# Projection stage: posts behind a tile's sums held back for a while, bank copies by priority; scan, sample states and output projection at other places in the order

## The chip, the cores and the metric

The kernel runs on one core of a Trainium2 chip. The metric is the device time of one execution in microseconds (us), as the median of the runs. The engines are named as in the profile: PE (TensorE matmul) and PEld (its weight loads), DVE (VectorE), ACT (ScalarE), POOL (GpSimd) and SP (SyncE), which here issues the transfers between the chip's memory (DRAM) and the on-chip buffer. Sums of matmuls land in banks of PSUM.

## The reference

One layer of a decoder step for 1024 new tokens of one sequence and 8 x 8 tokens of eight running sequences: a half-step SwiGLU FFN, a mixing block with two branches and gates, a second half-step FFN, and a final norm. Cut to what matters here:

```python
def token_mixing(hn, ...):
    proj = hn @ w_in                       # 1024 -> u 1024, z 2048, xbc 3072, dt 32, gates 2048
    u, z, xbc, dt_raw, gate_logits = ...
    branch_pool = pool_mix(u_ext, ...) @ pool_w_out   # mean of the last 2/4/8/16 rows minus u, a 256x256 map per group
    xbc_c, new_conv = causal_conv(xbc, conv_hist, conv_w, conv_b)   # width 4, SiLU
    dt = softplus(dt_raw + dt_bias); A = -exp(a_log)
    y, new_ssm = ssd_scan(xs, dt, A, bm, cm, ssm_h0)  # h_t = exp(dt A) h + dt x B^T, y = h C, by chunks of 128
    y = rmsnorm per group of ((y + d_skip * xs) * silu(z)) * ssd_norm
    branch_ssd = y @ ssd_w_out
    merged = sigmoid(g0) * branch_pool + sigmoid(g1) * branch_ssd
    return merged @ w_o, new_pool, new_conv, new_ssm

x = x + 0.5 * swiglu(rmsnorm(x), ffn1_w_in, ffn1_w_out)
x = x + mix
x = x + 0.5 * swiglu(rmsnorm(x), ffn2_w_in, ffn2_w_out)
```

All inputs and outputs are float32.

## The kernel before

**Numbers.** Float32 products are made of three matmuls of rounded halves: a value is split into its rounding and the rest (`wh` and `wl` for a weight, `hi`/`lo`, `fh`/`fl`, `mh`/`ml` and so on for an activation). ACT writes the rounding, DVE the rest (L443 and L444, L294 and L295 for weights; L355 and L357 or L359 for activations). Tokens come in two halves: h = 0 has 512 columns, h = 1 has 512 + 64, the 64 of the running sequences.

**Stages.** First FFN up to about 820 us; dt and some gates up to about 880; the projection up to about 1526; the mix (pooling branch, scan, output of the scan, merge, output projection) up to about 2150; second FFN to the end.

**Projection** (`in_proj`, `proj_pair`, lines 1052 to 1170). Columns of `w_in` are taken in pairs of tiles of 128: gates first, then four groups of three conv pairs c, one pooling pair u and two z pairs. A pair is computed by `wino` with seven products of half-size matrices in place of eight (`PRODUCTS`, in the order 1, 2, 6, 5, 7, 3, 4). Products add up in PSUM banks A, B and C of each half, and after each product `after(p, ...)` takes one bank's sums out: ACT copies them (`t` L1104, `v` L1109, `t` L1111 for half 0, L1088 to L1100 for half 1), or DVE or POOL adds them to what is there. A bank that is copied is written by a later product: product 6 needs the copy `t`, product 7 the copy `v`. Weights of some products are sums of weight tiles that POOL makes (L437).

When a tile of the pair is complete, `done()` appends its post-processing to the list `work`: for c the conv (ACT L933, DVE L937, SiLU on ACT L939), for u the window sums (DVE L952, L956, the difference from the mean L963 to L969 and the split of d: ACT `dh` L355, DVE L357), for z and g an activation (ACT L917, L912). A worker, a generator on a side chain, takes the list's first entry whenever it is free, and yields `POST` units between its parts; `proj_pair` steps it until at most three entries are left. `state_out` (transposes `pst` on PE, copies `so` on ACT) writes the new histories.

**Order.** Side chains are generators. Each yields a delay; a clock `pe[0]` of ideal PE time in us advances with the matmuls of the main stream, and `tick()` behind a few matmuls runs the chains whose time has come. The scheduler then puts each engine's instructions in an order of its own by priorities and their modelled readiness; instructions under `tc.high_priority(n)` go ahead by n. On the chip each engine works its queue in order.

**Mix.** `pool_branch` is main stream: a 256 x 256 map per group (`pgm`), then the pool output (`pbp`). Beside it `scan()` goes through groups and chunks by `ssd_group` with a delay `STEP[h]` between parts of a chunk: `ssd_a` (transposes `pxT`, decays `ab` by ACT's exponentials L1342 to L1345 and DVE's mask L1346, products `xdt`, `xd`), `ssd_st` (state sums `pst`), `ssd_b` (`pyd`, `pyo`, outputs; for the running sequences the states: `h0` loaded from DRAM, transposed as `ph0T` to `h0T`, and `pnew`). `sample_parts` makes the running sequences' factors for the states (`px3`, `pb3`). Norms (`rstd`) sum squares by matmul (`pss`). `ssd_out` (`pso`), `merge` (mh, ml) and `out_proj` (`pwo`, added to x at L1619) follow on the main stream for half 0 and then half 1. Two tags of PSUM banks are shared in this stage, "ps" and "pd".

Of the kernel before, what the change touches and what calls it, by code (L numbers as in the profile page):

```python
# [14 lines left out]
P = 128  # L15
# [28 lines left out]
STEP = (5.2, 4.1)  # L44
STEP_S = 1.0
POST = 1.0
GP = (1.0, 1.2)
# [14 lines left out]
def tile_hybrid_pool_ssd_macaron(  # L62
# [306 lines left out]
    def rstd(tiles, h, count, out, pace=1.0):  # L369
# [13 lines left out]
        yield max(pace, 1.5)  # L383
# [443 lines left out]
    def mix_dt(h, xs):  # L827
# [9 lines left out]
        def chain():  # L837
# [32 lines left out]
            yield 12  # L870
# [37 lines left out]
    work, hists, poster = [], {}, [None]  # L908
# [84 lines left out]
    def done(kind, i, h, raw):  # L993

        H, N = BEFORE[kind], NTOK[h]
        if kind in "zg":
            work.append((post_z if kind == "z" else post_gate)(h, i, raw[:, :N]))
            return
# [8 lines left out]
        if kind == "c":  # L1007
            if h == 1:
                smp = new
                state_out(kind, i, raw[:, 512:579])  # L1010
            work.append(post_conv(h, i, raw, smp))
        else:
            if h == 1:
                smp = hists.pop(("u", i))
                G.tensor_copy(smp[0][:, :, HIST:], new)
                state_out(kind, i, raw[:, 512:591])
            work.append(post_u(h, i, raw, smp))
# [6 lines left out]
    def state_out(kind, i, rows_):  # L1024
# [25 lines left out]
        work.append(put())  # L1050

    def proj_pair(kind, ia, ib, xs):
# [3 lines left out]
        while len(work) > 3:  # L1056
            poster[0].step()
        if kind == "u":
# [14 lines left out]
        def after(p, i, bk):  # L1073
# [9 lines left out]
            af, as_, bf, bs = a[:, H : H + n], a[:, H + n : H + 2 * n], b[:, H : H + n], b[:, H + n : H + 2 * n]  # L1083
            A, B, C = bk
# [36 lines left out]
            if p == "3":  # L1121
                done(kind, ia, h, a)
            elif p == "4":
                done(kind, ib, h, b)
# [3 lines left out]
    def in_proj(prep):  # L1128
# [24 lines left out]
        work.append(sample_hist())  # L1153
# [72 lines left out]
    def pool_branch(h):  # L1226
# [11 lines left out]
        for gi in range(4):  # L1238
# [3 lines left out]
            for j, pg in enumerate(dense2(wg[gi], 0, 0, [(h, dh, dl)], ("ps", "ps"), name="pgm")):  # L1242
# [26 lines left out]
    def sample_parts(g, xrs, dtd3):  # L1269

        out = []
        for i, xr in enumerate(xrs):
            px, pb = psum("ps", "px3"), psum("ps", "pb3")
            for j in range(4):
                tr(px[:96, j * P : (j + 1) * P], xr[:, j, :], ident)
            tr(pb[:96, :P], xr[:, 4, :], ident)
            xd, X3 = act((P, 512), name="xd3")[:96], act((P, 512), F32R, "X3")[:96]
            V.tensor_tensor(xd.rearrange("p (h d) -> p h d", d=HD), px[:96, :].rearrange("p (h d) -> p h d", d=HD),
                            dtd3[:, i, g * HPG : (g + 1) * HPG].unsqueeze(2).broadcast_to([96, HPG, HD]), op=ALU.mult)
            S.activation(X3, xd, AF.Copy)  # L1280
            V.tensor_tensor(X3[32:64], xd[32:64], X3[32:64].bitcast(F32), op=ALU.subtract)
            B3 = small((96, P), "B3", 1, F32R)
            S.activation(B3, pb[:96, :P], AF.Copy)
            V.tensor_tensor(B3[64:96], pb[64:96, :P], B3[64:96].bitcast(F32), op=ALU.subtract)
            bb = act((P, 4, P), F32R, "bblk")[:96]
            V.tensor_tensor(bb, B3.bitcast(F32).unsqueeze(1).broadcast_to([96, 4, P]),
                            bsel3.unsqueeze(2).broadcast_to([96, 4, P]), op=ALU.mult)
            out.append((X3, bb))
        return out

    def ssd_a(h, g, c, Bf, Cf, xs4, dts):
# [19 lines left out]
        if smp:  # L1311
            xrs = spread(Bf, xs4)
        yield
# [16 lines left out]
        if smp:  # L1330
            xd = sample_parts(g, xrs, cdp[1])
# [17 lines left out]
    def ssd_b(h, g, c, a, hold, Cf, y4, dts):  # L1349
# [8 lines left out]
        if smp:  # L1358
            units = [(pr, bh) for bh in range(2) for pr in range(4)]

            def src(u):
                gp = g * 4 + u[0]
                return state_ssm[0, u[1] * 4 : u[1] * 4 + 4, 2 * gp : 2 * gp + 2].rearrange("b h p n -> (h p) b n")

            def load(u):
                t = act((P, 4, P), name="h0")
                dma(t, src(u))
                return t
# [9 lines left out]
            h0s = {i: load(units[i]) for i in range(3)}  # L1378
            hTs = {}
            yield STEP_S  # L1380
            for i, (pr, bh) in enumerate(units):
                if i + 3 < len(units):
                    h0s[i + 3] = load(units[i + 3])
# [65 lines left out]
    def ssd_group(h, g, Bf, Cf, xs4, dts, zs):  # L1449
        y4 = xs4  # L1450
        prev = None
        step = STEP[h]
        for c in range(4 + h):
            ga = ssd_a(h, g, c, Bf, Cf, xs4, dts)
# [9 lines left out]
            try:  # L1464
                next(ga)
            except StopIteration as e:
                a = e.value
            yield step
            if prev:
                for w in ssd_b(h, g, *prev, Cf, y4, dts):  # L1470
                    yield w
            prev = (c, a)
        yield step
        for w in ssd_b(h, g, *prev, ssd_st(h, g, *prev, dts), Cf, y4, dts):
            yield w
# [134 lines left out]
    def out_proj(h, mh, ml):  # L1610
        N = NTOK[h]
        out = []
        for m in range(KD):
            x_ = act((P, N), name="x2")
            dma(x_, xspill[h][m])
            pw = dense(w_o[0], 0, KD, m * P, [(h, mh, ml)], name="pwo")[0]
            with tc.high_priority(HP_EV):
                for pt, (a, b) in zip(pw, PIECES[h]):
                    V.tensor_tensor(x_[:, a:b], x_[:, a:b], pt[:, : b - a], op=ALU.add)  # L1619
            dma(xspill[h][m], x_)  # L1620
            if h == 1:
                out.append(x_)
# [139 lines left out]
```

## Time and profile before

| | |
|---|---|
| median of 3 runs | 2939.78 us (2939.3 to 2945.45) |
| profiled execution, its own time | 2943.95 us |
| its span | 2942.2 us (1.75 us lie around it) |
| busy, share of the span | PE 96%, PEld 88%, DVE 60%, ACT 47%, POOL 34% |
| mean granted clock of PE | 0.989 |
| first FFN, 0 to 820 | PE busy 794.13 |
| dt and gates, 820 to 880 | PE busy 56.97 |
| projection, 880 to 1526 | PE busy 628.57, clock 0.99 |
| mix, 1526 to 2150 | PE busy 583.32, clock 0.97 |
| second FFN, 2150 to 2943 | PE busy 773.71 |

A row of the timeline has the start, the duration of one or the extent of several, engine, line, operation, output <- input by the program's names, shapes, count, and in brackets the engine's idle time before it with what ended it. A row of the waits has who waited for whom: total, times, longest. A row of the windows has the window, its length, busy times with numbers of instructions, PE's granted clock (1.00 is full speed), the DMA share and GB/s.

### The profile page before, as it was taken

The numbers are of one execution on the slowest core, as the hardware profiler recorded it, in microseconds if no ns is written. First come the engines' busy times: TensorE is split into PE (matmuls) and PEld (weight loads), VectorE is DVE, ScalarE is ACT, GpSimd is POOL, SyncE is SP. The second block draws the span as 40 slices with busy tenths as digits, with TensorE's granted clock in tenths as the row PEclk, the third lists the DMA queues.
The fourth block names the chain that finished last, engine by engine and source line by source line (L and its number), as shares of the span: only waits on it lengthen the run. The fifth ranks groups of instructions, "written<-read, shape, count | busy, mean of one in ns | idle before, by whom it ended". The sixth has DMA issues, their size and how long they took to land.

```text
span 2942.2 us, 51070 instructions
## 1 busy us (share of the span) xinstructions
PE 2836.7 (96%) x18494; PEld 2575.2 (88%) x18494; DVE 1779.3 (60%) x2843; ACT 1385.2 (47%) x3024; POOL 1001.0 (34%) x1011
## 2 busy tenths in 40 slices
PE   7999999999999999999988999889999999999998
PEld 6999999889989989898977987668999999988898
DVE  6655555434474687887866867865765554453422
ACT  5444444323344555554546656567334444443422
POOL 5444444000133355455522233322225444440000
PEclk9999999999999999999999999999999999999999
DMA  4575554856445455533368677776774432236652
GB/s 125 168 228 183 159 172 133 277 189 195 113 123 171 153 180 160 177 127 122 104 217 253 211 241 236 240 230 196 246 243 155 156 108 74 84 97 215 217 157 72
DMA packets 530332, 507.97 MB, mean 173 GB/s; under 512 B 36884, under 2 KB 374664, under 8 KB 530072
## 3 DMA queue, kind: packets, MB, share of 16 engines
q1 hardware_dynamic: 530064, 504.72, 53.8%
q8 instruction: 145, 2.38, 0.3%
q14 instruction: 107, 0.88, 0.1%
q10 hardware_dynamic: 16, 0.00, 0.0%
HBM read 361.77 MB, written 143.05 MB: 172 GB/s over the span
## 4 chain that ended last, share of the span: by engine, by line
PE 79%; DVE 9%; DMA 4%; ACT 4%; issue 2%; POOL 1%; SPq 1%; DVEq 0%; ACTq 0%; POOLq 0%
PE pw L163 42%; PE po L163 18%; PE pso L163 4%; PE pg L163 3%; PE pwo L163 2%; PE pbp L163 2%; PE pu L163 2%; DVE ct L937 1%; PE pyd L163 1%; DVE wl L444 1%; ACT ab L1344 1%; DMA t<-gd 1%; DVE us L952 1%; PE pst L163 1%; PE pyo L163 1%
## 5 line engine op out<-in xcount | busy, mean ns | idle before, releaser
L163 PE MATMUL pw<-X,wh 128*128 128x288 f32 (+1 forms) x2484 | 624.7, 330 | 12.1 <-ACT v L560 4.3
L163 PE MATMUL pw<-X,wl 128*128 128x288 f32 (+1 forms) x1644 | 474.0, 288 | 3.4 <-DVE wl L444 3.4
L163 PEld LDWEIGHTS pw<-X,wh 128*128 128x128 f32 x2484 | 419.0, 189 | 50.9 <-ACT v L560 5.2
L163 PE MATMUL pw<-hl,wh 128*128 128x512 f32 x1072 | 391.4, 399 | 1.9 <-DVE t L1113 0.9
L444 DVE TENSOR_TENSOR wl<-s,wh 128x512 fp32r<-128x512 f32 x288 | 225.4, 783 | 192.8 <-ACT wh L443 170.9
L163 PE MATMUL pw<-hi,wh 128*128 128x288 f32 x1120 | 331.0, 296 | 1.4 <-ACT t L596 1.3
L163 PE MATMUL pw<-lo,wh 128*128 128x288 f32 x1120 | 329.7, 294 | 0.0
L163 PE MATMUL pw<-hi,wl 128*128 128x288 f32 x1120 | 329.6, 294 | 0.0
L437 POOL TENSOR_TENSOR s<-wraw,wraw 128x512 f32<-128x512 f32 x144 | 206.6, 1435 | 325.3 <-DVE wl L444 216.2
L163 PEld LDWEIGHTS pw<-X,wl 128*128 128x128 f32 x1644 | 311.3, 189 | 5.4 <-DVE wl L444 5.4
L295 DVE TENSOR_TENSOR wl<-wraw,wh 128x512 fp32r<-128x512 f32 x228 | 163.6, 721 | 250.3 <-ACT wh L294 233.2
L163 PE MATMUL pw<-hl,wl 128*128 128x256 f32 x1072 | 299.8, 280 | 2.2 <-DVE wl L444 2.1
L294 ACT ACTIVATE wh<-wraw 128x512 fp32r<-128x512 f32 x228 | 137.7, 607 | 322.8 <-PE po L163 243.9
L444 DVE TENSOR_TENSOR wl<-wraw,wh 128x512 fp32r<-128x512 f32 x216 | 168.9, 782 | 135.5 <-ACT wh L443 127.9
L443 ACT ACTIVATE wh<-s 128x512 fp32r<-128x512 f32 x288 | 181.0, 629 | 139.3 <-PE pw L163 137.0
L163 PEld LDWEIGHTS pw<-hl,wh 128*128 128x128 f32 x1072 | 202.0, 188 | 39.5 <-DVE t L1113 1.4
L163 PEld LDWEIGHTS pw<-hi,wh 128*128 128x128 f32 x1120 | 210.0, 188 | 13.7 <-ACT t L596 1.9
L163 PE MATMUL po<-hh,wh 128*128 128x288 f32 (+1 forms) x800 | 210.9, 323 | 2.9 <-ACT hh L355 2.6
L163 PE MATMUL po<-hr,wh 128*128 128x288 f32 (+1 forms) x800 | 211.1, 323 | 0.0
L163 PE MATMUL po<-hh,wl 128*128 128x288 f32 (+1 forms) x800 | 210.7, 322 | 0.0
L163 PEld LDWEIGHTS pw<-lo,wh 128*128 128x128 f32 x1120 | 210.2, 188 | 0.0
L163 PEld LDWEIGHTS pw<-hi,wl 128*128 128x128 f32 x1120 | 210.1, 188 | 0.0
(384 smaller groups left out, 6346.8 us busy)
## 6 DMA issues: line engine op xcount, KB each, us to landing
wraw<-in_ffn_w_in_dram SPq DMA_DIRECT2D x188, 256.0 KB
wh<-part SPq DMA_DIRECT2D x156, 256.0 KB
wl<-part SPq DMA_DIRECT2D x156, 256.0 KB
wraw<-in_w_in_dram SPq DMA_DIRECT2D x144, 256.0 KB
wraw<-in_ffn_w_out_dram SPq DMA_DIRECT2D x120, 256.0 KB
part<-ph SPq DMA_DIRECT2D x80, 256.0 KB
part<-pr SPq DMA_DIRECT2D x80, 256.0 KB
ab<-acsd SPq DMA_DIRECT2D x64, 256.0 KB
```

Of the source, the lines that this page charges most:

```text
L163: T.matmul(out, lhsT, rhs, start=start, stop=stop, skip_group_check=free)
L294: S.activation(wh, raw, AF.Copy)
L295: V.tensor_tensor(wl, raw, wh.bitcast(F32), op=ALU.subtract)
L437: G.tensor_tensor(t, a, b, op=op)
L443: S.activation(wh, a, AF.Copy)
L444: V.tensor_tensor(wl, a, wh.bitcast(F32), op=ALU.subtract)
L937: V.scalar_tensor_tensor(o, f(j), w[j], o, op0=ALU.mult, op1=ALU.add)
L952: V.tensor_tensor(nx[:, 2 * sh - 1 : HIST + 512], cur[:, 2 * sh - 1 : HIST + 512], cur[:, sh - 1 : HIST + 512 - sh], op=ALU.add)
L1344: S.activation(ab[:L, i, :], ab[:L, i, :], AF.Relu, bias=acs[:L, hc + q * hq + i : hc + q * hq + i + 1], scale=-1.0)
```

## The change

It has five parts.

1. Projection. An entry of `work` is stamped with `pe[0] + RIPE` (3 units), and the worker takes it only from then on, unless the stage is ending or `proj_pair` is emptying the list; the list may hold four entries in place of three. The bank copies of `after` are moved into `leave` and put under `tc.high_priority(40)`.
2. Delays: `rstd` waits 2 x max(pace, 0.75) ahead of its sums in place of max(pace, 1.5), `GP`, `mix_dt` 16 for 12, `STEP` (5.0, 3.8) for (5.2, 4.1).
3. `pgm` takes its banks from "pd" in place of "ps".
4. Running sequences' parts of the scan: each `sample_part` is a step of its own with a delay `STEP_S` ahead, and the first three `h0` loads of a group are issued in `ssd_a` in place of `ssd_b`.
5. `out_proj`: the first two tiles m = 0, 1 go in turns by halves of K (kb = 0 for both, then kb = 4 for both), with `dense` written out.

```diff
-STEP = (5.2, 4.1)
+STEP = (5.0, 3.8)
-POST = 1.0
-GP = (1.0, 1.2)
+POST, RIPE = 1.0, 3.0
+GP = (1.5, 1.2)
...
-        yield max(pace, 1.5)
+        yield 2.0 * max(pace, 0.75)
         pt = psum("ps", "pss")
...
-            yield 12
+            yield 16
             pa = psum("ps", "pacs")
...
+    def post(gen):
+        work.append((pe[0] + RIPE, gen))
...
-            work.append(post_conv(h, i, raw, smp))
+            post(post_conv(h, i, raw, smp))
...
-        while len(work) > 3:
+        hurry[0] = True
+        while len(work) > 4:
             poster[0].step()
+        hurry[0] = False
...
+            A, B, C = bk
+            with tc.high_priority(HP):
+                leave(p, h, n, o, af, as_, bf, bs, A, B, C)
+            if p == "3":
+                done(kind, ia, h, a)
+            elif p == "4":
+                done(kind, ib, h, b)
...
         def worker():
             while work or not last[0]:
-                if work:
-                    yield from work.pop(0)
+                if work and (last[0] or hurry[0] or work[0][0] <= pe[0]):
+                    yield from work.pop(0)[1]
                 else:
                     yield 1.0
...
-            for j, pg in enumerate(dense2(wg[gi], 0, 0, [(h, dh, dl)], ("ps", "ps"), name="pgm")):
+            for j, pg in enumerate(dense2(wg[gi], 0, 0, [(h, dh, dl)], ("pd", "pd"), name="pgm")):
...
         if smp:
             xrs = spread(Bf, xs4)
+            h0s.update({i: load_state(g, u) for i, u in enumerate(UNITS[:3])})
         yield
...
         if smp:
-            xd = sample_parts(g, xrs, cdp[1])
+            xd = []
+            for i, xr in enumerate(xrs):
+                yield STEP_S
+                xd.append(sample_part(g, i, xr, cdp[1]))
...
-        for m in range(KD):
-            x_ = act((P, N), name="x2")
-            dma(x_, xspill[h][m])
-            pw = dense(w_o[0], 0, KD, m * P, [(h, mh, ml)], name="pwo")[0]
...
+        for ms in ((0, 1),) + tuple((m,) for m in range(2, KD)):
+            po = [banks([(h,)], "pd", "pwo")[0] for _ in ms]
...
+            for kb in (0, 4):
+                for m, pts in zip(ms, po):
+                    wh, wl = load_w(w_o[0], kb, 4, m * P)
+                    for kk in range(4):
+                        products([pts], wh, wl, kk, slice(0, P), [(h, mh, ml)], kb + kk, KD)
+                        tick()
```

What it moves, at three places. Lines from 1090 on are 16 higher in the changed kernel at the bank copies (L1104 is L1120), and 3 higher in the posts (L952 is L955).

ACT, first z pair behind the pooling pair of group 2; `t` and `v` are the copies of bank A, `ra` a copy of half 1, `dh` the rounding of the pooling pair's d. Before:

```order
L1104 COPY t_15471<-pw_2846_15460 128x512
L443 ACTIVATE wh_15603<-s_2874_15601 128x512
L1088 COPY ra_15490<-pw_2852_15477 128x288
L355 ACTIVATE dh_15528<-dd_15511 128x576
L1109 COPY v_15472<-pw_2846_15460 128x512
L1092 COPY ra_15490<-pw_2852_15477 128x288
```

and changed:

```order
L1120 COPY t_15468<-pw_2845_15457 128x512
L1104 COPY ra_15487<-pw_2851_15474 128x288
L443 ACTIVATE wh_15599<-s_2873_15597 128x512
L1125 COPY v_15469<-pw_2845_15457 128x512
L443 ACTIVATE wh_15637<-s_2878_15635 128x512
L1108 COPY ra_15487<-pw_2851_15474 128x288
L355 ACTIVATE dh_15545<-dd_15525 128x576
```

`dh` now stands behind `v` and the weight rounding and copy that follow it.

DVE, end of the first z pair of group 3: `ra` is the last sum of half 1 of a tile, `us` and `urs` are window sums of the pooling pair's post, `wl` on `wraw` is the rest of the next weight. Before:

```order
L1098 TENSOR_TENSOR ra_17091<-pw_3132_17185,ra_17091 128x288
L952 TENSOR_TENSOR us_17296<-rb_16796 128x526
L357 TENSOR_TENSOR dd_17232<-dd_17232,dh_17252 128x512
L952 TENSOR_TENSOR us_17312<-us_17296 128x524
L1120 TENSOR_TENSOR rb_17071<-pw_3106_17061,t_17072 128x256
L952 TENSOR_TENSOR us_17315<-us_17312 128x520
L956 TENSOR_TENSOR urs_16856<-urs_16856 128x8x16
L952 TENSOR_TENSOR us_17318<-us_17315 128x512
L444 TENSOR_TENSOR wl_17378<-wraw_17333,wh_17377 128x512
```

and changed:

```order
L1114 TENSOR_TENSOR ra_17088<-pw_3131_17183,ra_17088 128x288
L969 TENSOR_TENSOR dd_17248<-us_17230,invcnt 128x15
L444 TENSOR_TENSOR wl_17361<-wraw_17314,wh_17360 128x512
L970 TENSOR_TENSOR dd_17248<-dd_17248,rb_16770 128x15
L955 TENSOR_TENSOR us_17309<-rb_16794 128x526
L1136 TENSOR_TENSOR rb_17068<-pw_3105_17058,t_17069 128x256
```

The weight's rest now stands two places behind the sum, with one short instruction between, and the window sums behind it.

PE, start of the mix: `pgm` of the first groups, the first matmuls of `pbp`, and the first transposes `pxT` of the scan. Before:

```order
L163 MATMUL pgm_17841<-d_17579,wl_17826 128x512
L163 MATMUL pbp_17916<-fh_17749,wh_17918 128x512
L163 MATMUL pbp_17916<-fl_17750,wh_17918 128x512
L163 MATMUL pbp_17916<-fh_17749,wl_17919 128x512
L163 MATMUL pbp_17916<-fh_17784,wh_17918 128x512
L163 MATMUL pbp_17916<-fl_17785,wh_17918 128x512
L163 MATMUL pbp_17916<-fh_17784,wl_17919 128x512
L163 MATMUL pbp_17916<-fh_17801,wh_17918 128x512
L167 MATMUL pxT_17852<-ident,xs_3234_17757 128x128
L163 MATMUL pcb_17857<-bc_17756,bc_17755 128x128
```

and changed:

```order
L163 MATMUL pgm_17875<-d_17573,wl_17826 128x512
L167 MATMUL pxT_17841<-ident,xs_3234_17757 128x128
L163 MATMUL pcb_17846<-bc_17756,bc_17755 128x128
L167 MATMUL pcb_17846<-ident,bc_17755 128x128
L167 MATMUL pxT_17841<-ident,xs_3234_17757 128x128 x3
L163 MATMUL pgm_17892<-d_17816,wh_17887 128x512
```

The transposes now follow the 36th `pgm` matmul at once; seven `pbp` matmuls that stood between are behind them, and the last twelve of this part's `pgm` too, which had stood further on before as well.

More of the change, by code (lines that the diff above doesn't have):

```diff
@@ L1048, in put @@
                     dma(new_s[0, b, (7 if kind == "u" else 0) :, cd_], t[r1 - last_ : r1, cs])
-        work.append(put())
+        post(put())
     def proj_pair(kind, ia, ib, xs):
@@ L1267, in spread @@
         return out
[L1269 to L1289, printed above, removed]
@@ L1293, in ssd_a @@
+    def ssd_a(h, g, c, Bf, Cf, xs4, dts, h0s):
         dt, acs, dtd, cd, cdp = dts
@@ L1358, in ssd_b @@
         if smp:
[L1359 to L1368, printed above, removed]
+            units = UNITS
             def turn(h0):
```

76 lines of the change are left out of this document (48 added, 28 removed).

## The prediction

> **What bounds the kernel now.** I read the page's busy times first, then the same by stage (boundaries at 820, 880, 1526, 2150 us), then what TensorE (PE) waited for in the two stages that the change touches, and last the timeline at the longest waits.
>
> ```profile
> span 2942.2 us, 51070 instructions
> PE 2836.7 (96%) x18494; PEld 2575.2 (88%) x18494; DVE 1779.3 (60%) x2843; ACT 1385.2 (47%) x3024; POOL 1001.0 (34%) x1011
> ...
> 880.00:1526.00 646.00, 628.57 (x4160) 584.42 (x4158) 488.43 (x782) 348.55 (x704) 306.78 (x352) 0.99 0.47 151
> 1526.00:2150.00 624.00, 583.32 (x3946) 490.32 (x3947) 429.99 (x666) 361.42 (x922) 179.02 (x140) 0.97 0.74 236
> ```
>
> PE is the bound: busy 96%. The change adds no matmul, so all it can give is PE's idle time and time at a reduced clock. The columns behind the window are its length, busy time of PE, PEld, DVE, ACT, POOL, then granted clock, DMA share, GB/s. The projection (second row) has 17.4 us of idle PE, the mix (third row) 40.7, and there a mean clock of 0.97, worth 624 x 0.03 = 19 us more. Who ends these waits:
>
> ```profile
> PE pw L163 <- DVE wl L444: 5.6, 8, 1.9
> PE pw L163 <- ACT v L1109: 3.5, 2, 2.3
> PE pw L163 <- ACT t L1104: 3.3, 2, 2.5
> PE pst L167 <- DVE ra L1098: 2.9, 5, 1.3
> ...
> PE pss L163 <- DVE ssq L380: 5.7, 6, 2.7
> PE pgm L163 <- DVE fl L359: 3.7, 1, 3.7
> PE ph0T L167 <- DMA h<-in_state_ssm_dram: 2.7, 3, 1.9
> ...
> PE px L167 <- DVE xdt L1328: 2.1, 1, 2.1
> ```
>
> (Total, times, longest; first four projection, then mix.) In the projection PE waits for bank copies that stand behind other work in an engine's queue:
>
> ```profile
> 1347.90 0.68 DVE L963 SCALAR_TENSOR_TENSOR dd<-us,ra 128x512 f32<-128x512 f32 x1
> ...
> 1348.61 0.68 ACT L355 ACTIVATE dh<-dd 128x576 fp32r<-128x576 f32 x1 [6.59 <-DVE dd L963]
> 1349.20 0.57 ACT L1109 COPY v<-pw 128x512 f32<-128x512 f32 x1
> 1349.82 0.50 PE L163 MATMUL pw<-X,wh 128*128 128x512 f32 x1 [2.30 <-ACT v L1109]
> ...
> 1350.00:1353.40 3.40, 3.40 (x16) 3.17 (x17) 3.40 (x7) 1.90 (x5) 1.59 (x1) 0.66 0.52 196
> 1353.40:1356.00 2.60, 2.60 (x16) 2.43 (x15) 2.60 (x5) 0.42 (x1) 1.90 (x2) 0.79 0.33 95
> ```
>
> ACT sat 6.59 us on a rounding of d for which DVE was late, the copy v behind it was late, and PE idled 2.30 us. Behind it the granted clock falls to 0.66 and 0.79: 3.4 x 0.34 + 2.6 x 0.21 = 1.70 us more.
>
> **Part by part.** Sums are against the profiled execution: span 2942.2, whole 2943.95. It is 4.17 above the median of the runs, 2939.78, so I take 4.17 off at the end.
>
> *Projection.* At the 1349.82 place the order puts dh behind v on ACT: the wait and its clock loss go, **-4.0** (2.30 + 1.70; bound 0, if v then meets another late item). At the end of group 3 a weight rounding wl stands behind seven DVE instructions of the posts after L1098:
>
> ```profile
> 1491.19 0.44 DVE L1098 TENSOR_TENSOR ra<-pw,ra 128x288 f32<-128x288 f32 x1
> ...
> 1495.32 0.68 DVE L444 TENSOR_TENSOR wl<-wraw,wh 128x512 fp32r<-128x512 f32 x1
> 1496.06 0.39 PE L163 MATMUL pw<-hl,wl 128*128 128x256 f32 x1 [1.88 <-DVE wl L444]
> ...
> 1474.73 0.50 PE L163 MATMUL pw<-X,wh 128*128 128x512 f32 x1 [2.53 <-ACT t L1104]
> 1474.70:1478.00 3.30, 3.27 (x21) 3.08 (x22) 3.30 (x6) 0.83 (x3) 2.06 (x2) 1.00 0.45 164
> ```
>
> Now it stands two behind L1098, some 3.5 us earlier: **-1.9**. The 2.53 at 1474.73 stays, 0: on ACT dh still stands ahead of t there (bounds -2.5, and +1.7 if the wait, which left the clock at 1.00, grows into a clock loss). The other wl waits (5.6 - 1.9) and the pst waits (2.9, whose L1098 moves by one short instruction at most): the queues are reordered by one to three places, I take **-1.0**, between -6.6 and one new wait of the size 1.9. Held-back work must be done some time: GpSimd is busy 306.78 of 646, so it has room, but the last posts end later and the mix starts with their results: **+1.0** (0 to 2.3, the size of the wait at 1349.82).
>
> *Before the projection*, mix_dt's sums come four units of PE work later:
>
> ```profile
> 825.96 0.49 PE L163 MATMUL pacs<-dt,tri 128*128 128x128 f32 x2 [2.13 <-DVE dt L868]
> ```
>
> **-2.1** (bound 0).
>
> *Mix, start.* SP issues the first xs loads where it did, but pxT now stands ahead of seven pbp matmuls:
>
> ```profile
> 1534.34 0.39 PE L163 MATMUL pbp<-fh,wh 128*128 128x512 f32 x1
> 1534.57 0.39 PE L163 MATMUL pbp<-fl,wh 128*128 128x512 f32 x1
> ...
> 1538.32 0.30 PE L167 MATMUL pxT<-ident,xs 128*128 128x128 f32 x1 [2.23 <-DMA xs<-cv]
> ```
>
> 7 x 0.23 = **+1.6** on a wait that ends with a transfer; the clock loss there is paid already.
>
> *pgm banks and rstd.*
>
> ```profile
> 1605.13 1.02 PE L163 MATMUL pss<-ones,ssq 128*128 128x1 f32 x8 [2.71 <-DVE ssq L380]
> ...
> 1616.57 0.54 PE L163 MATMUL pgm<-d,wh 128*128 128x288 f32 x2 [3.74 <-DVE fl L359]
> ...
> 1617.00:1620.00 3.00, 3.00 (x15) 3.00 (x15) 3.00 (x7) 2.65 (x6) 0.00 (x0) 0.55 1.04 333
> ```
>
> The 3.74 is a wait for a "ps" bank, which pgm now does not use; its clock loss is 3 x 0.45 = 1.35. Since fl still is behind the scan's exponentials on ACT, I take **-3.0** of 5.1 (bound 0). pss is due later, but the scan is, too, ahead of where it was; by the order the first pss has as many pbp (192) before it as it had: **-1.0** of 5.7 (upper bound +2, an L380 more).
>
> *Sample states and out_proj.*
>
> ```profile
> 1971.82 0.63 PE L167 MATMUL px<-ident,xr 128*96 128x128 f32 x4 [2.15 <-DVE xdt L1328]
> 1973.93 0.32 SPq L1620 DMA_DIRECT2D xspill<-x  x1
> 1979.65 0.32 SPq L284 DMA_DIRECT2D wh<-part  x1
> 1980.06 2.03 SPq L1367 DMA_DIRECT2D h<-in_state_ssm_dram  x4
> 1972.00:1979.00 7.00, 6.82 (x38) 5.80 (x37) 6.75 (x12) 3.79 (x10) 0.00 (x0) 0.52 0.11 41
> ...
> 1869.08 0.50 PE L163 MATMUL pwo<-ml,wh 128*128 128x512 f32 x1 [2.25 <-DVE ml L359]
> 1869.00:1872.50 3.50, 3.42 (x10) 2.66 (x10) 3.50 (x6) 1.91 (x4) 0.93 (x1) 0.63 0.67 252
> ```
>
> SP stood from 1973.93 to 1979.65 at a weight load that waits for its buffer, and the state loads behind it (L1367) went out at 1980.06, too late for ph0T. With the first three issued at the start of ssd_a they are ahead of such a wait, and the second sample part no longer follows the first at once. That meets the ph0T wait (2.7), the px wait (2.1) and the clock loss (7 x 0.48 = 3.4): **-6.0** of 8.2 (bound 0). What is now behind the three loads on SP are weight loads and xspill writes; by the row above a load takes 2.03 / 4 = 0.5 us to issue, 1.5 for three, and the weights are loaded ahead, so I put nothing for it here and have it within the next term but one. In out_proj the second halves of mh, ml are needed 24 matmuls of 0.23 = 5.4 us later; the wait of 2.25 and its 3.5 x 0.37 = 1.3 of clock go, **-3.5** (bound 0).
>
> *Denser scan.* Steps of 5.0/3.8 for 5.2/4.1 bring the same chains (ACT 361.42 of 624, DMA share 0.74) in less of PE's work: new waits, **+4.0**, between 0 and the +23 of the second rival.
>
> Sum: -4.0 - 1.9 - 1.0 + 1.0 - 2.1 + 1.6 - 3.0 - 1.0 - 6.0 - 3.5 + 4.0 = -15.9. 2943.95 - 15.9 = 2928.05, less 4.17: **2924**.
>
> **A rule against part of this.** The clock fell behind waits of 2.25 and 2.30 us, but not behind 2.53. The Trainium skill ("TensorE: Matmul & The Clock Gate", Part 1 and its table of consequences) puts the fall behind at least one idle window of about 3.4 us, and asks for no idle gaps over about 3 us. By that rule the two falls have another cause and stay when the waits go, and the sum would be some 5.5 us smaller, as rival (3) works out from rows. The trace differs: it has falls right behind shorter waits, and I go by the trace.
>
> **The rivals.**
> (1) *Waits change places.* PE's idle time in the mix is set by the pace of DVE and ACT, not by where a wait stands: pgm, pss, sample and out_proj gains (13.5) come back elsewhere. For it: in the mix the longest entry among the waits is 5.7 of 40.7, so the idle time has many causes, each near its turn. Against: ACT and DVE are busy 58% and 69% there. -15.9 + 13.5 = -2.4: 2937. Chance 0.14.
> (2) *Slower: pyd waits for the exponentials.* By the order of PE the scan is ahead, by up to 13 us of PE work in the second half, and at the first pss pyd follows it at once, where 36 pgm stood between. Its operand comes by
>
> ```profile
> 1611.74 1.28 ACT L1344 ACTIVATE ab<-ab,dts 128x128 f32<-128x128 f32 x4
> ...
> 1613.23 0.61 ACT L1345 ACTIVATE ab<-ab 128x512 f32<-128x512 f32 x1
> ...
> 1613.87 0.69 DVE L1346 TENSOR_TENSOR ab<-ab,cbm 128x512 f32<-128x512 f32 x1 [2.30 <-ACT ab L1345]
> ```
>
> 1.28 + 0.61 + 0.69 = 2.6 us; exposed, with 1.3 of clock, 3.9 for each chunk. There are 36 chunks (four groups, four chunks in the first half, five in the second); without the +4.0 the sum is -19.9, so it turns to slower by over 0.2% (5.9) from seven on; at seven +7.4, 2947, and the 23 above is six of them. For it: DMA share 0.74, ACT in order. Against: ACT is busy 361 of the 624 us, and its chains are done ahead of PE wherever the waits above name another releaser. Chance 0.17.
> (3) *The clock falls whatever the short waits do.* For it: the 2.53 without a fall. Against: the falls behind 2.30, 2.25 and 3.74. Then only the waits go, and 1.70 + 1.3 + about half of 1.35 and 3.4, some 5.5, stay: 2929 (2924 + 5.5). Chance 0.09. The rule of the Trainium skill named above ("TensorE: Matmul & The Clock Gate", Part 1) is of this kind.
>
> **How the numbers follow.** Forecast 0.60. A measurement of this kernel can tell about 0.2%, 5.9 us, from no change. Faster: nearly all of the forecast and of (3), a little of (1): 0.69. Slower: most of (2): 0.16. Same: 0.15. With all waits at their favourable bounds the sum would be some 20 lower, which won't come together: low 2908. High 2945 takes in (1), (3) and (2) below six chunks.
>
> **What would show it.** Right: no wait on v at the u to z place of group 2, nor on wl at the end of group 3; mix with less than 34 us of PE idle and a clock above 0.975; px, ph0T together under 2; pwo behind ml gone; pxT at 3.8. Wrong: pyd or pso among the mix's first waits, ACT's dh or v longer in the projection, or the mix as long as before (624).

## The result, and the profile after

| | median, us | runs |
|---|---|---|
| before | 2943.47 | 20 (2938.22 to 2947.9) |
| changed | 2938.52 | 20 (19 from 2933.75 to 2941.21, one 3935.24) |
| ratio | 0.9983 | 95%: 0.9976 to 0.999 |

The one run at 3935.24 us had a granted clock of 0.654 and is a slow run; the ratio compares fast runs alone. The change takes 4.95 us, 0.17%, off the median. The forecast was 2924, with 15.9 us of gain; the median of three runs that it started from, 2939.78, was itself 3.7 below the median of twenty. The profiled execution after took 2939.05 us, against 2943.95 before. The page after, its busy times:

```profile
span 2937.3 us, 51029 instructions
PE 2828.8 (96%) x18494; PEld 2570.2 (88%) x18494; DVE 1784.7 (61%) x2843; ACT 1385.2 (47%) x3024; POOL 993.0 (34%) x1011
```

In these two profiles the span is 4.9 us shorter, PE's busy time 7.9 us (2836.7 before) for the same 18494 matmuls, and PE's idle time is 3.0 us longer. Windows cut at fixed times hide shifts of a few us, so here both kernels are cut at the same instructions: the first product of the projection, the first `pgm`, and the first `pg` of the second FFN. The columns are those of the prediction; the changed kernel has 15 matmuls more in the first row, since mix_dt's sums now fall into it. Before:

```profile
872.56:1526.07 653.51, 636.01 (x4211) 591.21 (x4209) 491.76 (x787) 351.96 (x712) 310.06 (x355) 0.99 0.47 152
1526.07:2182.84 656.77, 615.33 (x4184) 522.12 (x4185) 454.29 (x700) 371.10 (x938) 192.65 (x153) 0.97 0.74 237
```

After:

```profile
869.74:1523.04 653.30, 636.56 (x4226) 591.23 (x4224) 503.38 (x793) 352.17 (x716) 300.94 (x355) 1.00 0.47 152
1523.04:2176.96 653.92, 611.37 (x4184) 521.09 (x4185) 451.99 (x700) 371.48 (x938) 193.82 (x153) 0.97 0.74 238
```

Length less PE's busy time is PE's idle time: 17.5 and 41.4 us before, 16.7 and 42.6 after. So almost none of the idle time that the change was to remove is gone. Other profiles, of the runs below, say the same: in the mix PE idles 42.5 us in the mean of five profiles with the old order there (39.75 to 44.23) and 42.4 in the mean of nine with the new one (40.98 to 44.31); in the projection 17.5 to 19.05 in four with the old order and 16.5 to 18.1 in six with the new one. The waits of PE say why. After, projection (880 to 1526; total, times, longest):

```profile
PE pst L167 <- DVE ra L1114: 6.7, 8, 1.4
PE pw L163 <- ACT t L1120: 5.3, 5, 3.0
PE pw L163 <- DVE t L1129: 2.1, 2, 1.3
PE pw L163 <- DVE wl L444: 1.0, 3, 0.5
...
PE pw L163 <- ACT v L1125: 0.4, 1, 0.4
```

The two waits that the prediction removed are gone (v 3.5 to 0.4, wl 5.6 to 1.0, together 7.7). But pst rose from 2.9 to 6.7, ACT's t from 3.3 to 5.3, and DVE's t from 0.9 to 2.1: 7.0 came back. After, mix (1526 to 2150):

```profile
PE pst L163 <- DVE xd L1347: 6.5, 4, 4.0
PE pss L163 <- DVE ssq L380: 5.9, 3, 2.7
PE pxT L167 <- DMA xs<-cv: 4.4, 3, 3.6
PE pgm L163 <- DMA d<-dh: 4.3, 1, 4.3
PE pso L163 <- ACT acc L1577: 3.2, 1, 3.2
PE pwo L163 <- DVE t L1608: 3.1, 1, 3.1
PE pgm L163 <- DVE fl L359: 2.9, 3, 1.2
PE pyd L163 <- ACT btok L1336: 2.8, 2, 1.7
...
PE pwo L163 <- DVE ml L359: 0.9, 1, 0.9
...
PE px L167 <- DVE B L1294: 0.5, 1, 0.5
PE ph0T L167 <- DMA h<-in_state_ssm_dram: 0.2, 1, 0.2
```

The waits of before that the prediction named are shorter here, too: px 2.1 to 0.5, ph0T's on its load 2.7 to 0.2, pwo on ml 2.6 to 0.9. In their place stand pst on xd, pgm on d, pwo on t and pyd on btok, none of which stands in before's list. Three waits of the changed kernel at their places, first ACT's timeline at the end of a z pair (start, length, and in brackets the idle time ahead and what ended it):

```profile
1465.03 0.69 ACT L942 ACTIVATE ct<-ct 128x576 f32<-128x576 f32 x1 [2.83 <-DVE ct L940]
...
1471.96 0.63 ACT L355 ACTIVATE dh<-dd 128x512 fp32r<-128x512 f32 x1 [4.06 <-DVE dd L970]
1472.50 0.24 ACT L1039 COPY so<-pst 79x128 f32<-79x128 f32 x1
1472.64 0.58 ACT L1120 COPY t<-pw 128x512 f32<-128x512 f32 x1
```

Then PE behind each of the three waits, and DVE ahead of the third:

```profile
1473.28 0.79 PE L163 MATMUL pw<-X,wh 128*128 128x512 f32 x1 [2.98 <-ACT t L1120]
...
1542.59 0.77 PE L163 MATMUL pgm<-d,wh 128*128 128x512 f32 x1 [4.34 <-DMA d<-dh]
...
1874.46 0.67 DVE L1608 SCALAR_TENSOR_TENSOR t<-t,pso 128x512 f32<-128x512 f32 x1
...
1875.19 0.50 PE L163 MATMUL pwo<-mh,wh 128*128 128x512 f32 x1 [3.11 <-DVE t L1608]
```

At 1473 ACT stands 4.06 us at a rounding of d, as it did before the change (3.58), and the bank copy t stands behind it. At 1542 the last `pgm` products ask for a d whose load has not landed. At 1875 out_proj's two tiles want a bank each at once, and the first is freed only by the merge's t.

**Where the 5 us are.** In all profiles taken, by which program ran in a stage: dt and projection 733.5 us as before (3 profiles), 731.2 changed (5); mix 656.1 (652.4 to 659.9; 5) and 653.6 (651.6 to 654.6; 9). That is -2.3 and -2.5. In the mix the idle time has no part in it, as said above: the means differ in PE's busy time (613.5 and 611.2) for the same matmuls. The first FFN, which the change doesn't touch, varies by more from profile to profile (787.4 to 794.3), so where the 5 us come from stays open. The next two experiments couldn't split the sum further.

### The profile page after: what moved, and what is told of

It reads as the page before. It is cut to its first block, busy times and chain, and to the rows that moved or that the text cites. A ratio compares the mean times of both kernels' runs of the same rounds, so it can differ in the third digit from the quotient of the medians.

```text
span 2937.3 us, 51029 instructions
## 1 busy us (share of the span) xinstructions
PE 2828.8 (96%) x18494; PEld 2570.2 (88%) x18494; DVE 1784.7 (61%) x2843; ACT 1385.2 (47%) x3024; POOL 993.0 (34%) x1011
## 4 chain that ended last, share of the span: by engine, by line
PE 44%; DVE 6%; ACT 3%; DMA 3%; issue 1%; POOL 1%; SPq 1%; POOLq 0%; ACTq 0%; DVEq 0%
PE pw L163 19%; PE po L163 9%; PE pso L163 4%; PE pwo L163 3%; PE pbp L163 3%; PE pg L163 1%; PE pu L163 1%; ACT ab L1357 1%; PE pyd L163 1%; DVE wl L444 1%; DVE ct L940 1%; PE pst L163 1%; DMA wraw<-in_ffn_w_in_dram 0%; DVE xs L1504 0%; DVE ab L1359 0%
## 5 line engine op out<-in xcount | busy, mean ns | idle before, releaser
L295 DVE TENSOR_TENSOR wl<-wraw,wh 128x512 fp32r<-128x512 f32 x228 | 164.2, 721 | 249.2 <-ACT wh L294 236.9
L437 POOL TENSOR_TENSOR s<-wraw,wraw 128x512 f32<-128x512 f32 x144 | 196.0, 1361 | 333.7 <-DVE wl L444 216.7
L444 DVE TENSOR_TENSOR wl<-wraw,wh 128x512 fp32r<-128x512 f32 x216 | 177.0, 819 | 123.0 <-ACT wh L443 116.3
```

Of the source, the lines that this page charges most:

```text
L295: V.tensor_tensor(wl, raw, wh.bitcast(F32), op=ALU.subtract)
L437: G.tensor_tensor(t, a, b, op=op)
L444: V.tensor_tensor(wl, a, wh.bitcast(F32), op=ALU.subtract)
```

## The experiments

Two theories stood at the start. **A**: order alone changes which wait is seen, and PE's idle time in a stage stays. **B**: parts of the change gain what was said, and one part takes it back. Further on, F and H say that the load of DVE (F) or ACT (H) sets the mix's idle time, G that the chains' lengths do, J that it is what an in-order engine stands at. C, D and E are single causes, stated in the expectations that test them.

**Halves of the change.** p1_alone is before with the projection's part (entries held for RIPE, bank copies by priority in `leave`, a list of four in place of three); rest_alone is the changed kernel without it. The core of what the first adds and the second takes out:

```diff
+            post(post_conv(h, i, raw, smp))
...
+        while len(work) > 4:
...
+            with tc.high_priority(HP):
+                leave(p, h, n, o, af, as_, bf, bs, A, B, C)
...
+                if work and (last[0] or hurry[0] or work[0][0] <= pe[0]):
```

> The kernel before with the projection part alone (held-back posts, list of four, copies by priority). Theory A (waits change places: DVE's queue sets the pace in the projection, so a wait moved from one place comes back at another): 0 to -3 us, ratio 0.999 to 1.000, with PE's idle time in the projection at 15 to 18 us as in both kernels and pst's waits up near 6. Theory B (the projection part gives what was forecast, -6, and the mix eats it): ratio about 0.998.

> The changed kernel with the projection part undone: delays, pgm banks, sample states and output projection alone. Theory A: about -3 us, ratio 0.999, by less clock loss in the mix while PE's idle time there stays at 41 to 43. Theory B (the mix loses): ratio 1.000 or above.

p1_alone 1.0002 (0.9992 to 1.0013), rest_alone 1.0 (0.9991 to 1.0009). p1_alone has pst 6.5, t 5.2, v 0.2, and 17.45 us of idle PE in the projection: the waits changed places, as A has it. rest_alone has 43.25 idle in the mix. Neither half shows a gain or a loss that B could use: B wanted 0.998 for the first, and A's -3 us for the second didn't come either. All four new waits of the mix stand in rest_alone, too (pst on xd 6.6, pgm on d 4.3, pwo on t 3.1, pyd on btok 2.7).

**Halves of the projection's part**, priority_alone has of that diff the third and fourth line alone, holding_alone the other three:

> The kernel before with the copies' priority alone, without the held-back posts. Theory A (order alone does not change the sum of the projection's waits): idle PE in the projection 15 to 19. Rival (the priority is the part that gains and holding back loses): 12 or less.

> The kernel before with the held-back posts and the list of four alone, without the priority. Theory A: idle PE in the projection 15 to 19. Rival (holding back gains, priority loses): 12 or less.

Idle PE 20.05 and 17.0 us: priority alone is 1 us above what A allows, and neither is near the 12 of the rival. (Their times, 2950.13 and 2952.33, are one execution each. They lie above all ten of before on that chip, 2933.39 to 2947.23; one execution can't tell whether that is the kernel.) With priority alone the v wait stays at 3.7; with holding alone it is 0.2 and pst 5.9: the holding moved the wait.

**The pgm banks**

```diff
-[(h, dh, dl)], ("pd", "pd"), name="pgm")
+[(h, dh, dl)], ("ps", "ps"), name="pgm")
```

> The changed kernel with pgm's banks back at the tag ps. Theory C (the pd banks let the last twelve pgm of half 0 run ahead of pbp, into data that SP loads too late): the 4.3 us wait of pgm on d goes and the stretch at half clock at the start of the mix gets shorter, but a wait of about 3.7 on fl in half 1 comes back: net -2 to -5 against the changed kernel, ratio 0.9965 to 0.9975. Rival (the wait is only one of data that come late anyway, and pbp would wait for the same): no change, 0.998.

0.9988 (0.9979 to 0.9997), so C's gain didn't come. The 4.34 on d goes, fl is back at 3.4, pbp has waits of 2.8 and 2.4; mix idle 44.0. A wait was exchanged for others of its size.

**out_proj alone** is before with the last hunk of the diff:

```diff
+        for ms in ((0, 1),) + tuple((m,) for m in range(2, KD)):
```

> The kernel before with the output projection's part alone. Theory E (the second tile takes its PSUM bank 12 matmuls earlier, and that bank is still being read by the merge on DVE): the 2.25 us wait on ml goes and a wait of 2 to 4 us on the merge's t comes at the start of the output projection of half 0; net 0 to +1 us. Rival (the new wait of 3.1 in the changed kernel comes from the scan's or the norm's place): no wait on t, net -3 to -4.

Then the changed kernel with the second tile's bank in another pool:

```diff
-po = [banks([(h,)], "pd", "pwo")[0] for _ in ms]
+po = [banks([(h,)], "ps" if m == 1 else "pd", "pwo")[0] for m in ms]
```

> The changed kernel with the bank of the output projection's second tile from the tag ps in place of pd. Theory E: the 3.1 us wait on the merge's t falls under 0.5 and the time by 2 to 4 us against the changed kernel. Rival: the wait stays, or turns into one on another bank.

out_alone 1.0004 (0.999 to 1.0019): ml's wait is gone, pyd waits 3.58 for btok, and a pwo further on 4.3 for x (1.9 in before); E's wait of pwo on t did not come in this run. pso waits for t twice (1.76 and 1.81), but the same order of the mix has 2.2 to 5.4 us of such waits in before, p1_alone, priority_alone and holding_alone. out_bank 0.9992 (0.9982 to 1.0002); the wait stayed:

```profile
1876.57 0.50 PE L163 MATMUL pwo<-mh,wh 128*128 128x512 f32 x1 [3.12 <-DVE t L1608]
```

I had blamed the second tile's bank; that fell. By the rows it is the first tile's, freed by t on a DVE that in the changed kernel is busy 19.99 of the 20 us from 1860; no run moves that one.

**Samples alone**, in before:

```diff
+            h0s.update({i: load_state(g, u) for i, u in enumerate(UNITS[:3])})
...
+            for i, xr in enumerate(xrs):
+                yield STEP_S
+                xd.append(sample_part(g, i, xr, cdp[1]))
```

> The kernel before with the sample states' part alone. By the forecast's step the waits of px and ph0T (2.1 + 2.7, with ACT's xr 1.7) fall by 4 or more and no other wait takes their place: idle PE in the mix 36 to 38 for 41.4. Theory G: the waits go, and idle stays at 40 or above.

px falls to 0.5 and 0.7, ph0T to 1.0, and pss on ssq rises from 5.7 to 13.7; mix idle 44.3, not 36 to 38 (2944.25, one execution).

**Less work in the mix.** In the changed kernel, mix_no_mask leaves out the mask's multiply on DVE (first line below), mix_no_relu the Relu on ACT (the others; the exponential's scale is changed with it).

```diff
-            V.tensor_tensor(ab[:L], ab[:L], cbm[:L, :L]..., op=ALU.mult)
...
-            for i in range(hq):
-                S.activation(ab[:L, i, :], ab[:L, i, :], AF.Relu, ...)
-            S.activation(ab[:L], ab[:L], AF.Exp, scale=-1.0)
+            S.activation(ab[:L], ab[:L], AF.Exp, scale=-0.001)
```

> The changed kernel without the causal mask's multiplication on DVE in the mix (68 instructions of 0.7 us left out, some 48 us of DVE's 431 there). Theory F (the mix's idle time too is set by DVE's queue): idle PE in the mix falls from 42.6 to under 30. Theory G (it is set by lumps of the scan's steps and chains across engines): it falls by less than 6.

> The changed kernel without the clamp on ACT ahead of the scan's exponential (four instructions of 0.32 us left out for each half of a chunk, some 85 us of ACT's 362 in the mix; the decay factors are other numbers). Theory H (ACT's queue sets the pace in the mix): idle PE there falls from 42.6 to under 30. Theory G: it falls by less than 8, by the waits behind the chain of ab alone.

The mix, first without the mask, then without the Relu:

```profile
1523.01:2164.67 641.66, 608.39 (x4184) 520.39 (x4185) 404.39 (x632) 371.36 (x938) 187.93 (x153) 0.97 0.75 243
```

```profile
1518.90:2151.77 632.87, 602.30 (x4184) 515.37 (x4185) 449.58 (x700) 289.30 (x650) 198.27 (x153) 0.98 0.76 246
```

48 us less of DVE's work leave 33.3 us idle, 82 less of ACT's 30.6. F and H wanted under 30 and G a fall of less than 6 and 8, where 9.3 and 12.0 came: no one of F, G, H holds. Work of either engine counts, and neither alone is the bound; whether by its load or because the chain gets shorter, these two runs (one execution each) don't separate.

**Less work in the projection**: two of three conv taps on DVE left out, in the changed kernel and in before.

```diff
-for j in range(1, 4):
+for j in range(1, 2):
```

> The changed kernel with one tap of the conv on DVE in place of three (the other two are left out, so the conv's values are incomplete): 48 conv tiles lose two DVE instructions of 0.7 us each and, in half 1, two of 0.3 more, some 80 us of DVE work in the projection. Theory A (DVE's queue sets the pace there, waits only change places): PE's idle time in the projection falls from 16.7 to under 9 and the time by 7 to 15 us. Rival (the waits are latencies of chains across engines, whatever DVE's load): idle time stays at 14 or more.

> The kernel before with the same two taps left out. Theory A: idle in the projection falls under 9 here too, and the difference between the two kernels in that stage is within 2 us. Rival (priorities and held-back posts matter most where DVE has room): this one keeps 5 us or more of idle time over the other.

After, then before, both with one tap:

```profile
871.81:1503.26 631.45, 629.63 (x4226) 590.26 (x4224) 404.04 (x649) 359.00 (x716) 281.54 (x355) 1.00 0.49 158
```

```profile
870.23:1500.03 629.80, 627.15 (x4211) 588.58 (x4209) 416.12 (x643) 353.86 (x712) 278.21 (x355) 1.00 0.49 157
```

Idle PE 1.8 and 2.65, the stage 22 to 24 us shorter: without the two taps the order makes no difference, and about 15 of the 17 us of idle PE are gone. The edit takes work off DVE, and it shortens the conv's chain; the next runs take these apart.

**The same relief, moved and not dropped.** tap_moved makes one tap's product on ACT and adds it on GpSimd in the middle of the chain; tap_last has the product at the start, the add last and the SiLU four units behind it; sums_on_pool puts the window sums on GpSimd, with three units between two of them in place of one.

```diff
+            if j == 2:
+                S.activation(o2, f(j), AF.Copy, scale=w[j])
+                G.tensor_tensor(t[:, :N], t[:, :N], t2[:, :N], op=ALU.add)
...
-            V.tensor_tensor(nx[:, 2 * sh - 1 : HIST + 512], ...
+            G.tensor_tensor(nx[:, 2 * sh - 1 : HIST + 512], ...
```

> The changed kernel with the conv's third tap off DVE: ACT makes its product (one instruction per piece) and POOL adds it. That takes some 48 x 0.74 + 24 x 0.27 = 42 us of DVE work out of the projection and gives 30 to 40 to ACT and 65 to 85 to POOL (1.35 to 1.8 an addition). Theory A (DVE's queue sets the pace): idle PE in the projection falls from 16.7 to 5 to 11, the time by 6 to 14 us, ratio 0.994 to 0.996. Rival (POOL's additions slow DVE by as much, or the chain across three engines is late): idle stays at 14 or above, ratio 0.998 or more.

> The changed kernel with one tap of the conv off DVE as in the run with the moved tap, but with ACT's product made at the start and POOL's addition as the last step ahead of the SiLU, so that no DVE instruction waits for POOL. Theory J (PE's waits come from what stands in front of a sum in DVE's in-order queue: the moved tap lost because DVE waited in front of the sums for POOL, and the two taps left out gained because nothing stood there): idle PE in the projection falls from 16.7 to 6 to 12, ratio 0.994 to 0.997. Rival (any work given to POOL slows DVE through the operands they share): idle stays above 16, ratio above 0.998.

> The changed kernel with the pooling pair's window sums on POOL in place of DVE (some 40 of 0.7 us and, in half 1, their sample parts), with three units between two sums. Theory J: the waits at the u to z places (2.98 on t, 1.26 and 0.89 on DVE's t) change with the place of dd in DVE's queue: if dd now waits for POOL in front of sums, idle rises above 20 as with the moved tap; if it stands late enough, it falls to 10 to 14. Rival (DVE's load alone): it falls to 10 to 14 whatever DVE waits for.

Slower: 1.0126 (1.0101 to 1.0151), 1.01 (1.0083 to 1.0116), 1.0027 (1.0016 to 1.0038). tap_moved's projection, and what DVE and ACT wait for in it (1000 to 1500 us):

```profile
870.69:1564.28 693.59, 651.10 (x4226) 602.28 (x4224) 470.69 (x721) 386.01 (x788) 361.31 (x403) 0.98 0.45 143
```

```profile
DVE ct L947 <- POOL ct L943: 49.9, 37, 3.3
...
ACT ct L949 <- DVE ct L947: 95.0, 41, 5.7
```

DVE has 33 us less to do, and PE's idle time is 42.5, not 2. So DVE's load alone is not what counts. What PE waits for shows what does, in tap_moved:

```profile
PE pst L167 <- DVE ra L1121: 22.9, 11, 3.0
PE pw L163 <- ACT ra L1115: 7.7, 4, 3.5
```

and in tap_last:

```profile
PE pw L163 <- ACT t L1125: 9.5, 6, 2.8
PE pst L167 <- DVE ra L1119: 6.9, 6, 2.4
PE pw L163 <- ACT v L1130: 6.5, 5, 1.8
...
ACT ct L947 <- POOL ct L945: 103.3, 47, 5.1
```

In tap_moved DVE stands in its queue for GpSimd (49.9 us), and what grows most is PE's wait for DVE's sums (22.9, where the changed kernel has 6.7). In tap_last no DVE step of the conv waits for GpSimd any more and that wait is back at 6.9; ACT stands 103.3 us at the SiLU, and PE waits for the copies behind it (t 5.3 to 9.5, v 0.4 to 6.5). So most of PE's new waits are for the engine that was made to stand. J as it was stated for tap_last had DVE's queue alone and expected 6 to 12 us of idle PE; 34.0 came, and ACT's queue was added to J afterwards. sums_on_pool has 19.9, which is neither J's "above 20" nor the 10 to 14 of DVE's load.

**pst's bank asked for later** (changed kernel):

```diff
+            yield 3.0
             pt = psum("ps", "pst8")
```

> The changed kernel with the transposes pst of the new histories three units later, so that eight or more matmuls of the next product stand between the last sum and the transpose. Theory D (PE stands because the transpose follows at once on the sum that it reads): pst's waits, 6.7 in all, fall below 1 and the time by 4 to 6 us, ratio 0.9963 to 0.997. Theory A (waits change places): PE's idle time in the projection stays at 15 to 18, ratio 0.998.

0.9981 (0.9972 to 0.999), no different from the change. pst's 6.7 are gone, and

```profile
PE pw L163 <- ACT t L1121: 10.8, 4, 3.4
```

took their place; idle 15.8. A again.

**The last steps of the posts held back.** last_steps_later puts the conv's SiLU and the rounding of u's d, with their DMAs, into chains that wait for 5 units more; later_with_pst has pst's delay in addition.

```diff
-        S.activation(t[:, :N], t[:, :N], AF.Silu)
-        dma(convd[h][ct], t[:, :N])
+        def last_step():
+            S.activation(t[:, :N], t[:, :N], AF.Silu)
+            dma(convd[h][ct], t[:, :N])
+        tails.append(later(5.0, last_step))
```

> The changed kernel with the last step of a post (the conv's SiLU on ACT, the split of the pooling pair's d on ACT and DVE) on a chain of its own, five units later, so that ACT has more of its own work in front of it. In ACT's order the SiLU stands 7.0 instructions behind the tile's first conv step on the mean in place of 6.3. Theory J (PE's waits follow the time that ACT and DVE stand in their queues for each other's post): ACT's standing for the conv, 63 us between 1000 and 1500, falls to 40 to 55, idle PE in the projection from 16.7 to 10 to 15, ratio 0.9965 to 0.998. Rival (theory A without a cause: any order gives 16 to 19): idle stays, ratio 0.998 to 0.999.

> The same, and the transposes pst three units later as in the run before. The candidate for a kernel that beats both. Theory J: pst's waits go, and since ACT stands less, the waits on t do not take their place in full as they did there (10.8): idle PE in the projection 8 to 13, ratio 0.995 to 0.9975. Rival: idle 15 to 18, ratio about 0.998.

Alone it is slower, 1.0027 (1.0013 to 1.004): ACT stands 76.2 us, where 40 to 55 were expected, and PE idles 20.7, where 10 to 15 were. With pst's delay it is **0.9963 (0.995 to 0.9975)**, 2930.79 against 2942.31 of before on the same chip: faster than before, and its interval lies just below that of the change; no run has these two side by side. Its projection, PE's waits and ACT's longest:

```profile
868.51:1513.12 644.61, 634.04 (x4227) 589.58 (x4225) 491.34 (x794) 354.28 (x716) 321.88 (x355) 1.00 0.48 154
```

```profile
PE pw L163 <- DVE wl L444: 2.5, 5, 0.7
PE pw L163 <- DVE t L1139: 2.3, 3, 1.3
PE pw L163 <- ACT t L1130: 1.8, 4, 0.9
...
ACT ct L945 <- DVE ct L941: 56.0, 33, 3.8
```

Idle 10.6 us, as expected (8 to 13), and no wait over 1.3. So A's claim that order alone doesn't change the idle time falls: of two further orders one gives 20.7, another 10.6. ACT's standing at the conv's step (us, 1000 to 1500), beside PE's idle time in the projection:

| kernel | ACT stands | PE idle |
|---|---|---|
| taps_after | 7.7 | 1.8 |
| taps_before | 25.6 | 2.65 |
| later_with_pst | 56.0 | 10.6 |
| pst_later | 59.0 | 15.8 |
| changed | 63.4 | 16.7 |
| p1_alone | 63.7 | 17.45 |
| before | 64.7 | 17.5 |
| rest_alone | 65.0 | 17.5 |
| sums_on_pool | 65.6 | 19.9 |
| priority_alone | 66.3 | 20.05 |
| holding_alone | 67.0 | 17.0 |
| last_steps_later | 76.2 | 20.7 |
| tap_moved | 95.0 | 42.5 |
| tap_last | 103.3 | 34.0 |

The low end, the middle and the high end lie as J has it. Inside the high end tap_moved and tap_last are in reverse order, and the eight from 59.0 to 67.0 lie within 4.3 us, where profiles of one projection differ by up to 1.6, so their order tells little. It is a correlation: no run changed the standing and nothing else, and DVE's standing is not in it. In before and changed it is 64.7 and 63.4: the change left it as it was.

## Why the prediction was wrong

The size was missed by a factor of three. That the sign was right and 2938.5 is inside 2908 to 2945 is luck as far as the runs show: the idle time that was to go is still there, and where the 5 us come from is open. The step that failed is the sum itself: each wait removed was booked as net gain, with a correction of +4.0 for new ones. What happened is rival (1), waits change places (2937, chance 0.14), and in the projection as well, where the rival had not put it: PE's idle time there went from 17.5 to 16.7, and in the mix, where under 34 was the sign of being right, from 41.4 to 42.6. A second step failed with it: the clock losses (1.70, 1.35, 3.4 and 1.3), read behind one wait of one profile each and booked as part of that wait.

- *Projection, -4.0 and -1.9.* Mechanism right for the waits, at both places: no wait of that size on v, and wl down by 4.6. The 1.70 of clock in the first term is no fixed price: behind the same wait (2.26 to 2.30) the clock was 0.66 in before and 0.63 in rest_alone, but 1.00 in out_alone and samples_alone. The next term, "other wl and pst, -1.0", had bounds of -6.6 and +1.9. What is left there: wl -2.7 beyond the 1.9, pst +3.8, ACT's t +2.0, DVE's t +1.2, together +4.3. The bound was the size of one wait; three groups of waits grew.
- *The 2.53 at 1474.73.* It was put at 0. It stands at 2.98 after, with the clock at 0.54 in the 3.3 us behind it, where it had been 1.00; so in this profile its upper bound came.

```profile
1473.20:1476.50 3.30, 3.22 (x11) 2.84 (x12) 3.30 (x6) 0.84 (x3) 1.57 (x2) 0.54 0.42 159
```

But six profiles have this projection, and in three of them the clock stayed at 1.00 behind the same wait:

| kernel | wait on t, us | clock in the 3.3 us behind |
|---|---|---|
| pgm_back | 2.98 | 0.51 |
| changed | 2.98 | 0.54 |
| mix_no_relu | 3.00 | 0.73 |
| mix_no_mask | 2.98 | 1.00 |
| out_bank | 3.00 | 1.00 |
| p1_alone | 2.95 | 1.00 |

- *dt, -2.1.* The wait on dt is gone; `pg` on wl beside it went from 0.8 to 2.7, so 0.2 of it remained as a gain.
- *pxT, +1.6.* Right: 2.23 became 3.65.
- *pgm banks, -3.0.* The 3.74 for a bank is gone, and 4.34 for d came: the bank had hidden that the last `pgm` products are ahead of their load. fl kept 2.9.
- *pss, -1.0.* 5.7 became 5.9.
- *Samples -6.0, out_proj -3.5.* The waits went nearly as said: px has 0.5 and ph0T 1.6 left (1.4 of it on DVE's h), where under 2 together was the sign. samples_alone and out_alone show that they don't count by themselves: pss took the one, pyd on btok and pwo on x the other.
- *Denser scan, +4.0.* Mis-sized, as the only term for new waits in the mix: pst on xd 6.5, pgm on d 4.3, pwo on t 3.1, pyd on btok 2.8 are 16.7 us, inside the 0 to 23 but four times the value. Not all of it is the denser scan's: the 4.3 belongs to pgm's banks, and btok's wait came in out_alone, too. No run has the delays alone; the 6.5 and the 3.1, which neither samples_alone nor out_alone has, are already more than twice the term.
- *Rival (2).* pyd is among the mix's waits, at 2.8 and for btok, not for the exponentials: it decides nothing here. pso, the other sign of being wrong, waits 3.2 in all, less than before (6.2).
- *Clock.* It was to be above 0.975 in the mix, and stayed at 0.97. But the mix of before ran in p1_alone as well, the same program there:

```profile
1519.79:2172.97 653.18, 608.95 (x4185) 516.81 (x4185) 454.11 (x700) 372.18 (x938) 195.34 (x153) 0.98 0.75 239
```

Summed over windows of 1 us, the time at the halved clock is about 37 us in before and about 20 in this run. So a clock loss read at one place of one profile is no fixed property of the wait ahead of it, as the two waits of the projection show place by place. The Trainium skill ("TensorE: Matmul & The Clock Gate", Part 1) says that the window which decides it runs freely, so that its phase differs from run to run; the two runs agree with that. Its other half, that about 3.4 us of idleness are needed, is not what 2.98 at 1473 shows.

## What to carry to other kernels

In this kernel the idle time of the bound engine behind in-order queues did not go with the wait in which it was seen: price a reordering by what each queue still stands at afterwards, and give the removed wait no value until that is named. Leaving work out first (two of three taps: idle 16.7 to 1.8) tells which work makes the idle time; moving one tap to other engines took load off DVE, put waits between engines into the chain, and lost (1.0126 and 1.01). Two edits that left the change's figure (0.9981 for 0.9983) or made it worse (1.0027) alone gave 0.9963 together, so a neutral edit isn't out before its partner is tried.

## What the hardware showed

An instruction of DVE that runs beside one of GpSimd on SBUF data can take more than twice as long. DVE's and GpSimd's timeline in the changed kernel, three like roundings and the GpSimd operation beside the second:

```profile
1191.71 0.69 DVE L444 TENSOR_TENSOR wl<-s,wh 128x512 fp32r<-128x512 f32 x1
1192.53 1.68 POOL L437 TENSOR_TENSOR s<-wraw,s 128x512 f32<-128x512 f32 x1 [2.07 <-issue]
1192.97 1.78 DVE L444 TENSOR_TENSOR wl<-wraw,wh 128x512 fp32r<-128x512 f32 x1
1197.64 0.68 DVE L444 TENSOR_TENSOR wl<-wraw,wh 128x512 fp32r<-128x512 f32 x1
```

The second begins inside the GpSimd operation and takes 1.78 us, the others 0.69 and 0.68. Between 1000 and 1500 us the 76 such roundings with no GpSimd operation beside them took 0.68 to 0.70 us each. The Trainium skill ("SBUF — State Buffer", section "Who interferes with whom") has a VectorE instruction with two inputs in SBUF contend with a GpSimd one that reads SBUF; this row agrees. In tap_last's projection,

```profile
870.68:1551.54 680.86, 646.83 (x4226) 597.12 (x4225) 486.32 (x721) 385.18 (x788) 369.23 (x403) 0.99 0.46 146
```

DVE needs 486.32 us for 721 instructions, the changed kernel 503.38 for 793: 9% fewer instructions, but only 3.4% less time, with GpSimd at 369 us instead of 301. A tap taken off DVE gave back little there; how much of that is this contention, no run separates.
